# Weight tiles of a block in two halves, 128 bytes apart modulo 256, with the K tiles sorted by the slot parity of their activations

## The chip, the cores and the metric

The kernel runs on one core of one Trainium2 chip. TensorE (PE) multiplies, VectorE (DVE), ScalarE (ACT) and GpSimd (POOL) work element by element, SyncE (SP) issues most of the DMAs. SBUF is the on-chip memory of 128 partitions; a tile has the same byte address in all of them, and the addresses below are those bytes within a partition. Metric: device time in microseconds (us) of one execution, the median over several.

## The reference

One decoder layer for 256 tokens of width 2048, with 16 meta tokens put in front (272 tokens, batch 1, everything in float32):

```python
q, c_kv, q_idx, k_idx, w_idx, u = split_columns(h @ w_in[l])
c_kv = rms_norm(c_kv, kv_norm_g[l])
o_lat = dsa_attention(q_abs, c_kv, q_idx, k_idx, w_idx, rel_bias, top_k)   # top-64 keys per query
pool_out = multiscale_pool(u, w_pool[l], pool_scale[l])
mix = jnp.concatenate([attn_out, pool_out], axis=-1) @ w_o[l]
h = layer_norm(ALPHA * h + mix, ln1_g[l], ln1_b[l])
f = conv_gated_ffn(h, w_up[l], conv_w[l], conv_b[l], w_down[l])   # 2048 -> 2 x 5632 -> 2048
h = layer_norm(ALPHA * h + f, ln2_g[l], ln2_b[l])
```

The large products have K = 2048 (the projections with 24 column blocks of 128 beside the first 336 columns, `w_o` with 16, `w_up` with 88) or K = 5632 (`w_down`).

## The kernel before

Each fp32 matrix is split into a high and a low part of type fp32r (`split_part`, L114 on ACT writes the high part, L115 on DVE the rest), activations and weights alike. A product of a 128 x 128 weight tile with the activations then takes three matmuls: high x high (L219), high x low (L220), low x high (L221). `product` runs them for the 16 K tiles of a block, one K tile after the other: 48 matmuls into one PSUM tile. In these products the weights are the stationary operand, loaded by an LDWEIGHTS of 128 columns ahead of each matmul (engine PEld in the profile), and the activations stream through in 256 to 272 columns. While one matmul streams, the weights of the next are loaded.

The weights come as a stream of blocks of 128 x 2048 floats (1 MB each), in this order: 8 blocks of indexer queries ("qi"), `w_uk` and `w_uv`, 8 blocks of attention queries ("q"), 8 blocks of pool channels ("u"), 16 of `w_o` ("o"), then 88 of `w_up` with the blocks of `w_down` between them (`ffn_plan`). `weights` fetches two blocks ahead: `fetch` (L118) issues one DMA on SP's queue into a tile `wraw` and splits it in two pieces of 1024 columns. The first 4 x 2 blocks of `w_up` multiply `folded` (the attention result before its norm is finished, 260 columns), the other 80 multiply `h_parts` (`hp`, 258 columns). Most of `w_down` runs through a seven-product scheme (`seven`, L812 to L814), where the weights stream in 512 columns and the activations are stationary.

Where things lie:

- `split_tile` (L138) gives a weight block a tile `whl` of 2 parts x 2064 floats, 16,512 bytes. That is 64.5 x 256, so the three buffers of the tag lie at 192, 64 and 192 modulo 256. The low part lies 8,256 bytes (64 modulo 256) behind the high part. K tile k lies at column 128 k, so 512 k bytes further: all 16 K tiles of a block lie alike modulo 256.
- After the three buffers comes a tile `gap` of 64 bytes, then a ring of 24 slots for activations of 2 parts x 272 floats, 2,176 bytes each. That is 8.5 x 256, so slots with an even number lie at 128 and those with an odd number at 0 modulo 256. The low part again lies 64 further.
- The framework picks the slots by which is free. In the built program of the kernel before, x's K tile 0 has slot 0 and K tile k slot 24 - k; `mix` 0 to 15 have the slots 8, 7, 6, 3, 2, 23, 22, 19, 18, 17, 21, 20, 1, 0, 5, 4; `hp` 0 to 15 have 16, 15, 14, 13, 12, 11, 10, 9, 5, 4, 1, 0, 21, 20, 8, 7.
- The qi products read x from column 16 on (64 bytes in), the q products from column 14 (56 bytes), the u products from column 12, 10, 6 or 0. `mix` and `hp` are read from their start. `folded` lies in another pool, in tiles of 2,080 bytes (32 modulo 256 from one to the next).

The order on each engine is set by the framework's scheduler from the order of the program text and from dependences. `output` (L644) reads `mix` in the fixed order 14, 15, 12, 13, 10, 11, 0 to 9; everywhere else the K tiles run from 0 to 15. The last two of `hp` are written (`normalise`, L726, high part L732 on ACT, low part L733 on DVE) while the first product on `hp` runs.

Of the kernel before, what the change touches and what calls it, by code (L numbers as in the profile page):

```python
# [11 lines left out]
F32 = mybir.dt.float32  # L12
F32R = mybir.dt.float32r
# [4 lines left out]
P = 128  # L18
D = 2048
NM = 16  # L20
S = 256
T = NM + S
Q0 = NM - 2
# [28 lines left out]
def ffn_plan():  # L52

    plan, f0 = [], 0
    for part, n in enumerate(PARTS):
        ups = [("up", f, half_) for f in range(f0, f0 + n) for half_ in range(2)]
        downs = []
        if part:
            chunks = 1 if part - 1 == FAST else 2
            downs = [(kind, part - 1, c, j) for c in range(chunks) for kind in "AB" for j in range(PARTS[part - 1] // 2)]  # L60
        while ups or downs:
            plan += ups[:1] + downs[:1]
            ups, downs = ups[1:], downs[1:]
        f0 += n
    return plan + [("down", FAST, c, g) for c in (1, 3) for g in range(PARTS[FAST] // 4)]


@with_exitstack
def tile_layer(ctx, tc, xt, w_first, w_proj, w_uk, w_uv, w_pool, w_o, w_up, w_down, cols, rows, rel_bias, onehot, out):
# [80 lines left out]
    def emit(i):  # L150
        if i in ready:
            return
        if i == last:

            raw = wp.tile([P, 2048], F32, tag="wraw", name="wraw")
            nc.sync.dma_start(raw, stream[i])
            raws[i] = raw
            ready[i] = []
            for c in range(0, 2048, 256):
                hl = ring.tile([P, 2, 258], F32R, tag="act", name="whl_r", padded_shape=[P, 2, T])  # L160
                nc.scalar.activation(hl[:, 0, :256], raw[:, c:c + 256], AF.Copy)
                nc.vector.tensor_tensor(hl[:, 1, :256], raw[:, c:c + 256], hl[:, 0, :256].bitcast(F32), op=ALU.subtract)
                ready[i].append(hl)
            return
        if i == spare:
            raw = wp.tile([P, 2048], F32, tag="wraw", name="wraw")
            hl = sb.tile([P, 2, 2048 + 2], F32R, tag="y", name="whl_y")
# [30 lines left out]
    def pieces(hl, a, b):  # L198
# [3 lines left out]
            return [(slice(c - a, e - a), hl[c // 256][:, 0, :e - c], hl[c // 256][:, 1, :e - c]) for c, e in cuts]  # L202
        return [(slice(0, b - a), hl[:, 0, a:b], hl[:, 1, a:b])]

    def row_sums(i, hl):

        total = sb.tile([P, 1], F32, name=f"total{i}")
        nc.scalar.activation(raws[i], raws[i], AF.Copy, accum_out=total)
        hi, lo = (hl[-1][:, p, 256:] if isinstance(hl, list) else hl[:, p, 2048:] for p in range(2))
        nc.scalar.activation(hi, total.to_broadcast([P, 2]), AF.Copy)  # L210
        nc.vector.tensor_tensor(lo, total.to_broadcast([P, 2]), hi.bitcast(F32), op=ALU.subtract)

    def product(ps, hl, m, act, lo, hi, ks=range(KT), width=P, k0=0, k1=KT):

        for n in range(k0, k1):
            k = ks[n]
            wh, wl = hl[:, 0, k * width:k * width + m], hl[:, 1, k * width:k * width + m]
            ah, al = act[k][:, 0, lo:hi], act[k][:, 1, lo:hi]
            nc.tensor.matmul(ps, wh, ah, start=n == 0, stop=False)  # L219
            nc.tensor.matmul(ps, wh, al, start=False, stop=False)  # L220
            nc.tensor.matmul(ps, wl, ah, start=False, stop=n == KT - 1)  # L221
# [169 lines left out]
    for j in range(8):  # L391
        hl = weights()
        ps = big()
        product(ps[:, :S], hl, P, x_parts, NM, T, k1=9)
        if j:
            pa_ = small()
            dots(j - 1, qis[j - 1], pa_, (0,))
        product(ps[:, :S], hl, P, x_parts, NM, T, k0=9, k1=12)
        if j:
            dots(j - 1, qis[j - 1], pa_, (1,))  # L400
        product(ps[:, :S], hl, P, x_parts, NM, T, k0=12)
# [81 lines left out]
    for h in range(H):  # L483
        hl = weights()
        ps = big()
        product(ps[:, :NQ], hl, P, x_parts, Q0, T)
        nc.scalar.activation(qt[:, h, :], ps[:, :NQ], AF.Copy)


# [122 lines left out]
    for h in range(H):  # L612
        g, j = 3 - h // 2, h % 2
        if j == 0:
            df = ap_.tile([P, 2, 2, NQ], F32R, name="df", tag="df")
        hl = weights()
        ps = big()
        product(ps[:, :T - starts[g]], hl, P, x_parts, starts[g], T, k1=4)
        if h == 0:
            meta_weights()  # L620
        lg_next = softmax(h + 1) if h + 1 < H else None
        product(ps[:, :T - starts[g]], hl, P, x_parts, starts[g], T, k0=4, k1=7)
        if turned:
            values(h - 1, *turned)
        product(ps[:, :T - starts[g]], hl, P, x_parts, starts[g], T, k0=7, k1=9)
        turned = turn(h, lg)
        product(ps[:, :T - starts[g]], hl, P, x_parts, starts[g], T, k0=9, k1=12)
# [6 lines left out]
        product(ps[:, :T - starts[g]], hl, P, x_parts, starts[g], T, k0=12)  # L634
        mean = trailing_mean(g, j, df, ps)
        if j == 1:
            late = (g, df, wpl)
        lg = lg_next
# [5 lines left out]
    def output(m):  # L644
        hl = weights()
        ps = big()
        product(ps[:, :NQ], hl, P, mix, 0, NQ, ks=order, k1=6 if m == 0 else KT)
        if m == 0:
            values(H - 1, *turned)
            less_token(*mean)  # L650
            product(ps[:, :NQ], hl, P, mix, 0, NQ, ks=order, k0=6, k1=14)
            pooled(*late)
            product(ps[:, :NQ], hl, P, mix, 0, NQ, ks=order, k0=14)
# [192 lines left out]
    for item in plan:  # L846
# [48 lines left out]
        if f < FOLDED:  # L895
            k = 0
            if f + half_ == 0:
                product(ps[:, :NE], hl, P, folded, 0, NE, k1=5)
                deviation()
                k = 5  # L900
            product(ps[:, :NE], hl, P, folded, 0, NE, k0=k)
# [209 lines left out]
```

## Time and profile before

| | |
|---|---|
| median of 3 runs | 1042.71 us (1042.28 to 1043.3) |
| profiled execution | 1042.3 us, of which its span is 1040.4 us |
| mean granted TensorE clock | 0.998 |
| PE busy | 1032.5 us (99%) |
| DVE busy | 890.4 us (86%) |
| ACT busy | 619.9 us (60%) |
| HBM read | 232.50 MB |

The span runs from the first instruction to the last one; the profiled execution's own time lies 1.9 us above it. Durations of matmuls overlap, since they are pipelined and their ends are modelled: a matmul's row shows 282 ns, but the next starts some 120 ns later. What a matmul costs is therefore read from start to start, in the timeline.

### The profile page before, as it was taken

The numbers are of one execution on the slowest core, as the hardware profiler recorded it, in microseconds if no ns is written. First come the engines' busy times: TensorE is split into PE (matmuls) and PEld (weight loads), VectorE is DVE, ScalarE is ACT, GpSimd is POOL, SyncE is SP. The second block draws the span as 40 slices with busy tenths as digits, with TensorE's granted clock in tenths as the row PEclk, the third lists the DMA queues.
The fourth block names the chain that finished last, engine by engine and source line by source line (L and its number), as shares of the span: only waits on it lengthen the run. The fifth ranks groups of instructions, "written<-read, shape, count | busy, mean of one in ns | idle before, by whom it ended". The sixth has DMA issues, their size and how long they took to land.

```text
span 1040.4 us, 19199 instructions
## 1 busy us (share of the span) xinstructions
PE 1032.5 (99%) x7644; PEld 984.0 (95%) x7644; DVE 890.4 (86%) x1401; ACT 619.9 (60%) x1000; POOL 186.1 (18%) x245
## 2 busy tenths in 40 slices
PE   9999999999999999999999999999999999999997
PEld 8999999999999999999999999999999999999986
DVE  6879568758779998888999999989898999999876
ACT  7656446645439855555665556655556565556675
POOL 1200014125330021121121111211112101120031
PEclk9999999999999999999999999999999999999999
DMA  9755643354553578989887798877988778888765
GB/s 326 256 183 202 237 145 126 139 194 163 179 194 129 197 224 239 276 282 301 275 276 264 268 294 276 279 264 270 291 279 276 266 280 277 277 274 280 288 218 156
DMA packets 59754, 250.28 MB, mean 241 GB/s; under 512 B 21734, under 2 KB 22416, under 8 KB 32656
## 3 DMA queue, kind: packets, MB, share of 16 engines
q1 hardware_dynamic: 34592, 230.42, 61.4%
q0 software_dynamic: 7888, 16.14, 8.3%
q10 hardware_dynamic: 17184, 2.49, 1.5%
q8 instruction: 60, 0.98, 0.4%
q14 instruction: 30, 0.25, 0.1%
HBM read 232.50 MB, written 2.11 MB: 225 GB/s over the span
## 4 chain that ended last, share of the span: by engine, by line
PE 94%; issue 2%; DMA 1%; DVE 1%; POOL 1%; ACT 0%; SPq 0%; POOLq 0%; DVEq 0%; ACTq 0%
PE mm L220 24%; PE mm L219 24%; PE mm L221 23%; PE at L814 6%; PE at L812 6%; PE at L813 6%; PE mm L291 2%; DMA wraw<-in_w_down 1%; DVE whl L115 1%; POOL gb L931 0%; DMA wraw<-in_w_first 0%; PE mm L519 0%; PE at L554 0%; PE at L381 0%; PE at L380 0%
## 5 line engine op out<-in xcount | busy, mean ns | idle before, releaser
L115 DVE TENSOR_TENSOR whl<-wraw,whl 128x1024 fp32r<-128x1024 f32 (+1 forms) x416 | 486.4, 1203 | 40.7 <-ACT whl L114 40.1
L114 ACT ACTIVATE whl<-wraw 128x1024 fp32r<-128x1024 f32 (+1 forms) x416 | 402.5, 1014 | 102.3 <-DMA wraw<-in_w_up 25.1
L220 PE MATMUL mm<-hp,whl 128*128 128x258 f32 x1280 | 364.3, 285 | 0.0
L219 PE MATMUL mm<-hp,whl 128*128 128x258 f32 x1280 | 361.0, 282 | 0.0
L221 PE MATMUL mm<-hp,whl 128*128 128x258 f32 x1280 | 360.3, 282 | 0.0
L219 PEld LDWEIGHTS mm<-hp,whl 128*128 128x128 f32 x1280 | 242.5, 189 | 3.1
L220 PEld LDWEIGHTS mm<-hp,whl 128*128 128x128 f32 x1280 | 241.6, 189 | 3.4 <-DVE hp L733 0.2
L221 PEld LDWEIGHTS mm<-hp,whl 128*128 128x128 f32 x1280 | 243.4, 190 | 0.2
L219 PE MATMUL mm<-xp,whl 128*128 128x256 f32 (+5 forms) x384 | 112.2, 292 | 0.0
L220 PE MATMUL mm<-xp,whl 128*128 128x256 f32 (+5 forms) x384 | 109.0, 284 | 0.0
L221 PE MATMUL mm<-xp,whl 128*128 128x256 f32 (+5 forms) x384 | 108.8, 283 | 0.0
L747 ACT ACTIVATE z<-mm,cv 128x256 f32<-128x256 f32 x40 | 22.6, 564 | 99.4 <-PE mm L221 97.8
L784 POOL TENSOR_TENSOR forms<-za 128x128 f32<-128x128 f32 x20 | 21.8, 1091 | 312.5 <-DVE za L765 246.0
L219 PEld LDWEIGHTS mm<-xp,whl 128*128 128x128 f32 x384 | 72.5, 189 | 1.0 <-issue 0.5
L220 PEld LDWEIGHTS mm<-xp,whl 128*128 128x128 f32 x384 | 72.4, 189 | 0.4
L221 PEld LDWEIGHTS mm<-xp,whl 128*128 128x128 f32 x384 | 72.4, 188 | 0.0
L747 ACT ACTIVATE za<-mm,cv 128x256 f32<-128x256 f32 x40 | 22.6, 564 | 81.7 <-PE mm L221 74.0
L814 PE MATMUL at<-whl,gp 128*128 128x512 f32 x180 | 71.0, 395 | 0.0
L813 PE MATMUL at<-whl,gp 128*128 128x512 f32 x180 | 70.7, 394 | 0.0
L812 PE MATMUL at<-whl,gp 128*128 128x512 f32 x180 | 69.3, 395 | 0.0
L787 POOL TENSOR_TENSOR forms<-za 128x128 f32<-128x128 f32 x20 | 19.4, 972 | 198.9 <-DVE za L765 184.9
L814 PEld LDWEIGHTS at<-whl,gp 128*128 128x128 f32 x180 | 33.8, 188 | 7.9
(349 smaller groups left out, 1886.7 us busy)
## 6 DMA issues: line engine op xcount, KB each, us to landing
wraw<-in_w_up SPq DMA_DIRECT2D x88, 1024.0 KB, 5.1
wraw<-in_w_down SPq DMA_DIRECT2D x80, 1024.0 KB, 6.6
wraw<-in_w_proj SPq DMA_DIRECT2D x24, 1024.0 KB, 5.1
wraw<-in_w_o SPq DMA_DIRECT2D x16, 1024.0 KB, 4.9
y<-v POOLq DMA_DIRECT2D x27, 256.0 KB, 7.7
y<-u POOLq DMA_DIRECT2D x18, 256.0 KB, 4.9
wraw<-in_w_first SPq DMA_DIRECT2D x8, 304.0 KB, 5.3
x<-in_xt SPq DMA_DIRECT2D x1, 2176.0 KB, 8.1
```

What stands on the lines that cost most here:

```text
L114: upper = nc.scalar.activation(hl[:, 0, c], raw[:, c], AF.Copy)
L115: lower = nc.vector.tensor_tensor(hl[:, 1, c], raw[:, c], hl[:, 0, c].bitcast(F32), op=ALU.subtract)
L219: nc.tensor.matmul(ps, wh, ah, start=n == 0, stop=False)
L220: nc.tensor.matmul(ps, wh, al, start=False, stop=False)
L221: nc.tensor.matmul(ps, wl, ah, start=False, stop=n == KT - 1)
L291: nc.tensor.matmul(ps[:m, :T], hl[:, t // 2, a0 + a:a0 + a + m], x_parts[k][:, t % 2, :], start=k == 0 and t == 0, stop=k == KT - 1 and t ...
L747: nc.scalar.activation(z, src[:, 2:NQ], AF.Identity, bias=col(C_B, j), scale=col(C_W, 3 * j + 2))
L784: nc.gpsimd.tensor_tensor(s[:, 0], a21, a22, op=ALU.add)
L787: nc.gpsimd.tensor_tensor(s[:, 3], a11, a21, op=ALU.subtract)
L812: nc.tensor.matmul(ps, a[:, 0, i], hl[:, 0, w], start=j == 0, stop=False)
L813: nc.tensor.matmul(ps, a[:, 0, i], hl[:, 1, w], start=False, stop=False)
L814: nc.tensor.matmul(ps, a[:, 1, i], hl[:, 0, w], start=False, stop=j == n - 1)
```

## The change

The change concerns `whl` and the order of K tiles in it.

- `whl` becomes 2 halves x 2 parts x 1040 floats, 16,640 bytes (65 x 256), so all three buffers lie alike modulo 256. The second half begins 8,320 bytes (128 modulo 256) behind the first, the low part 4,160 bytes (64 modulo 256) behind the high part. A small class `Split` lets the code index it as before.
- The host orders the K tiles of `w_proj`, `w_o` and `w_up` by three lists. The first eight of a list lie in the first half, the others in the second. In `K_O` and `K_UP` the first eight are the K tiles whose activations have even slots; in `K_PROJ` they are those with odd slots.
- `product` takes the list (`places`) to find a tile and by default also runs in its order. `output` keeps its order; the last of the u products keeps 0 to 15; the first product on `hp` runs in the order of `K_UP` with 14 and 15 last (`late_last`).
- The first stage (L243 ff.) places its six weight pieces of a buffer three to a half.
- To make room, `lm` shares the tag of `work`, and the four sums of `row_sums` share a tile `totals`. That moves the weight buffers and the ring: 96 bytes fewer stand ahead of them, and each weight buffer is 128 bytes larger.

The number of instructions, DMAs and bytes stays what it was.

```diff
+class Split:
+    def __init__(self, tile):
+        self.tile = tile
+    def __getitem__(self, key):
+        rows, part, c = key
+        a, b = c.start, 2 * 1024 + 2 if c.stop is None else c.stop
+        at = int(a >= 1024)
+        assert b <= 1024 or at == 1
+        return self.tile[rows, at, part, a - 1024 * at:b - 1024 * at]
+
+K_PROJ = (1, 3, 5, 7, 9, 11, 13, 15, 0, 2, 4, 6, 8, 10, 12, 14)
+K_O = (0, 2, 4, 6, 8, 11, 13, 15, 1, 3, 5, 7, 9, 10, 12, 14)
+K_UP = (0, 2, 4, 6, 9, 11, 13, 14, 1, 3, 5, 7, 8, 10, 12, 15)
...
-        hl = wp.tile([P, 2, 2048 + 2], F32R, tag="whl", name="whl", padded_shape=[P, 2, 2064])
+        hl = Split(wp.tile([P, 2, 2, 1024 + 16], F32R, tag="whl", name="whl"))
...
+    totals, totalled = sb.tile([P, 4], F32, name="totals"), []
+
     def row_sums(i, hl):
-        total = sb.tile([P, 1], F32, name=f"total{i}")
+        total = totals[:, len(totalled):len(totalled) + 1]
+        totalled.append(i)
...
-    def product(ps, hl, m, act, lo, hi, ks=range(KT), width=P, k0=0, k1=KT):
+    def product(ps, hl, act, lo, hi, places, ks=None, k0=0, k1=KT):
         for n in range(k0, k1):
-            k = ks[n]
-            wh, wl = hl[:, 0, k * width:k * width + m], hl[:, 1, k * width:k * width + m]
+            k = (places if ks is None else ks)[n]
+            w = slice(P * places.index(k), P * places.index(k) + P)
+            wh, wl = hl[:, 0, w], hl[:, 1, w]
...
-            xk, wk, c = raw[:, k % 3, :T], raw[:, k % 3, T:], slice(k % 6 * MF, k % 6 * MF + MF)
+            xk, wk, a0 = raw[:, k % 3, :T], raw[:, k % 3, T:], k % 6 // 3 * 1024 + k % 3 * MF
+            c = slice(a0, a0 + MF)
...
-    work = ap_.tile([P, KW], F32, name="work")
+    work = ap_.tile([P, KW], F32, name="work", tag="work")
...
-    lm = ap_.tile([2, H, NM], F32, name="lm")
+    lm = ap_.tile([P, KW], F32, name="lm", tag="work")[:2, :H * NM].rearrange("p (a b) -> p a b", b=NM)
...
+        ks = range(KT) if h == H - 1 else None
+        product(ps[:, :T - starts[g]], hl, x_parts, starts[g], T, K_PROJ, ks, k1=4)
...
-        product(ps[:, :NQ], hl, P, mix, 0, NQ, ks=order, k1=6 if m == 0 else KT)
+        product(ps[:, :NQ], hl, mix, 0, NQ, K_O, ks=order, k1=6 if m == 0 else KT)
...
+    late_last = [k for k in K_UP if k < 14] + [14, 15]
...
-            product(ps[:, :NQ], hl, P, h_parts, 0, NQ)
+            product(ps[:, :NQ], hl, h_parts, 0, NQ, K_UP, ks=late_last if f == FOLDED else None)
...
-    def blocks(w):
+    def blocks(w, places):
         k, m = w.shape
-        return np.ascontiguousarray(w.reshape(k // P, P, m // P, P).transpose(2, 1, 0, 3)).reshape(m // P, P, k)
+        w = w.reshape(k // P, P, m // P, P)[list(places)]
+        return np.ascontiguousarray(w.transpose(2, 1, 0, 3)).reshape(m // P, P, k)
```

More of the change, by code (lines that the diff above doesn't have):

```diff
@@ L166, in emit @@
             raw = wp.tile([P, 2048], F32, tag="wraw", name="wraw")
-            hl = sb.tile([P, 2, 2048 + 2], F32R, tag="y", name="whl_y")
+            hl = Split(sb.tile([P, 2, 2, 1024 + 16], F32R, tag="y", name="whl_y"))
         else:
@@ L393, in tile_layer @@
         ps = big()
-        product(ps[:, :S], hl, P, x_parts, NM, T, k1=9)
+        product(ps[:, :S], hl, x_parts, NM, T, K_PROJ, k1=9)
         if j:
@@ L397, in tile_layer @@
             dots(j - 1, qis[j - 1], pa_, (0,))
-        product(ps[:, :S], hl, P, x_parts, NM, T, k0=9, k1=12)
+        product(ps[:, :S], hl, x_parts, NM, T, K_PROJ, k0=9, k1=12)
         if j:
             dots(j - 1, qis[j - 1], pa_, (1,))
-        product(ps[:, :S], hl, P, x_parts, NM, T, k0=12)
+        product(ps[:, :S], hl, x_parts, NM, T, K_PROJ, k0=12)
         qi = queries[:, j % 2]
@@ L485, in tile_layer @@
         ps = big()
-        product(ps[:, :NQ], hl, P, x_parts, Q0, T)
+        product(ps[:, :NQ], hl, x_parts, Q0, T, K_PROJ)
         nc.scalar.activation(qt[:, h, :], ps[:, :NQ], AF.Copy)
@@ L617, in tile_layer @@
         ps = big()
-        product(ps[:, :T - starts[g]], hl, P, x_parts, starts[g], T, k1=4)
+        ks = range(KT) if h == H - 1 else None
+        product(ps[:, :T - starts[g]], hl, x_parts, starts[g], T, K_PROJ, ks, k1=4)
         if h == 0:
@@ L621, in tile_layer @@
         lg_next = softmax(h + 1) if h + 1 < H else None
-        product(ps[:, :T - starts[g]], hl, P, x_parts, starts[g], T, k0=4, k1=7)
+        product(ps[:, :T - starts[g]], hl, x_parts, starts[g], T, K_PROJ, ks, k0=4, k1=7)
         if turned:
             values(h - 1, *turned)
-        product(ps[:, :T - starts[g]], hl, P, x_parts, starts[g], T, k0=7, k1=9)
+        product(ps[:, :T - starts[g]], hl, x_parts, starts[g], T, K_PROJ, ks, k0=7, k1=9)
         turned = turn(h, lg)
-        product(ps[:, :T - starts[g]], hl, P, x_parts, starts[g], T, k0=9, k1=12)
+        product(ps[:, :T - starts[g]], hl, x_parts, starts[g], T, K_PROJ, ks, k0=9, k1=12)
         if j == 1:
@@ L633, in tile_layer @@
             less_token(*mean)
-        product(ps[:, :T - starts[g]], hl, P, x_parts, starts[g], T, k0=12)
+        product(ps[:, :T - starts[g]], hl, x_parts, starts[g], T, K_PROJ, ks, k0=12)
         mean = trailing_mean(g, j, df, ps)
@@ L650, in output @@
             less_token(*mean)
-            product(ps[:, :NQ], hl, P, mix, 0, NQ, ks=order, k0=6, k1=14)
+            product(ps[:, :NQ], hl, mix, 0, NQ, K_O, ks=order, k0=6, k1=14)
             pooled(*late)
-            product(ps[:, :NQ], hl, P, mix, 0, NQ, ks=order, k0=14)
+            product(ps[:, :NQ], hl, mix, 0, NQ, K_O, ks=order, k0=14)
         yd = y[:, m, Q0:]
@@ L897, in tile_layer @@
             if f + half_ == 0:
-                product(ps[:, :NE], hl, P, folded, 0, NE, k1=5)
+                product(ps[:, :NE], hl, folded, 0, NE, K_UP, k1=5)
                 deviation()
                 k = 5
-            product(ps[:, :NE], hl, P, folded, 0, NE, k0=k)
+            product(ps[:, :NE], hl, folded, 0, NE, K_UP, k0=k)
             with behind(state["use"]):
@@ L1085 @@
         "w_first": np.concatenate([tokens.T.reshape(KT, P, T), first.reshape(KT, P, MF)], axis=2),
-        "w_proj": blocks(np.concatenate([qi, q] + [u[:, 256 * g:256 * g + 256] for g in (3, 2, 1, 0)], axis=1)),
+        "w_proj": blocks(np.concatenate([qi, q] + [u[:, 256 * g:256 * g + 256] for g in (3, 2, 1, 0)], axis=1), K_PROJ),
         "w_uk": a["w_uk"][0].reshape(2, P, 1024).transpose(1, 0, 2).reshape(P, 2048),
@@ L1089 @@
         "w_pool": a["w_pool"][0].reshape(4, 2, P, 256).transpose(0, 2, 1, 3).reshape(4, P, 512),
-        "w_o": blocks(a["w_o"][0]),
-        "w_up": blocks(a["w_up"][0]),
+        "w_o": blocks(a["w_o"][0], K_O),
+        "w_up": blocks(a["w_up"][0], K_UP),
         "w_down": np.concatenate(down, axis=0),
```

## The prediction

> **What bounds the kernel.** I read the page's busy times and its chain of waits first, then a window over the long feed-forward stretch, then PE's groups of instructions, and last PE's timeline row by row.
>
> ```profile
> PE 1032.5 (99%) x7644; PEld 984.0 (95%) x7644; DVE 890.4 (86%) x1401; ACT 619.9 (60%) x1000; POOL 186.1 (18%) x245
> PE 94%; issue 2%; DMA 1%; DVE 1%; POOL 1%; ACT 0%; SPq 0%; POOLq 0%; DVEq 0%; ACTq 0%
> ```
>
> ```profile
> 350.00:1004.00 654.00, 653.96 (x4674) 617.17 (x4673) 596.96 (x843) 388.99 (x557) 104.67 (x125) 1.00 0.82 272
> ```
>
> In the window the columns are the stretch, its length, then busy us of PE, PEld, DVE, ACT and POOL, the granted clock, DMA share and GB/s. PE is on 94% of the chain and without a gap in 654 us, at full clock: a nanosecond less per matmul is a nanosecond less in the span, as long as DVE (596.96 of 654, 91%) and the DMAs (0.82) follow. So the question is only what a matmul costs from start to start.
>
> ```profile
> L220 PE MATMUL mm<-hp,whl 128*128 128x258 f32 x1280 | 364.3, 285 | 0.0
> L219 PE MATMUL mm<-hp,whl 128*128 128x258 f32 x1280 | 361.0, 282 | 0.0
> L221 PE MATMUL mm<-hp,whl 128*128 128x258 f32 x1280 | 360.3, 282 | 0.0
> L219 PE MATMUL mm<-xp,whl 128*128 128x256 f32 (+5 forms) x384 | 112.2, 292 | 0.0
> L220 PE MATMUL mm<-mixa,whl 128*128 128x258 f32 x128 | 36.5, 285 | 0.0
> L813 PE MATMUL at<-whl,gp 128*128 128x512 f32 x180 | 70.7, 394 | 0.0
> ```
>
> The products on `hp` are 80 blocks of 16 K steps of three matmuls; those on x and on `mix` (half `mixa`, half `mixp`) are 24 and 16 blocks. Now two successive `hp` products in the timeline, the first matmul of each K step (start us, us, the rest names it). The first product's weights lie in a buffer at 192 modulo 256:
>
> ```profile
> 897.58 0.28 PE L219 MATMUL mm<-hp,whl 128*128 128x258 f32 x1
> ...
> 897.94 0.28 PE L219 MATMUL mm<-hp,whl 128*128 128x258 f32 x1
> ...
> 898.29 0.29 PE L219 MATMUL mm<-hp,whl 128*128 128x258 f32 x1
> ...
> 898.66 0.28 PE L219 MATMUL mm<-hp,whl 128*128 128x258 f32 x1
> ...
> 899.02 0.28 PE L219 MATMUL mm<-hp,whl 128*128 128x258 f32 x1
> ...
> 899.38 0.28 PE L219 MATMUL mm<-hp,whl 128*128 128x258 f32 x1
> ...
> 899.74 0.28 PE L219 MATMUL mm<-hp,whl 128*128 128x258 f32 x1
> ...
> 900.10 0.28 PE L219 MATMUL mm<-hp,whl 128*128 128x258 f32 x1
> ...
> 900.45 0.28 PE L219 MATMUL mm<-hp,whl 128*128 128x258 f32 x1
> ```
>
> The second product's weights lie in the middle buffer, at 64:
>
> ```profile
> 905.43 0.28 PE L219 MATMUL mm<-hp,whl 128*128 128x258 f32 x1
> ...
> 905.78 0.29 PE L219 MATMUL mm<-hp,whl 128*128 128x258 f32 x1
> ...
> 906.15 0.28 PE L219 MATMUL mm<-hp,whl 128*128 128x258 f32 x1
> ...
> 906.51 0.28 PE L219 MATMUL mm<-hp,whl 128*128 128x258 f32 x1
> ...
> 906.87 0.28 PE L219 MATMUL mm<-hp,whl 128*128 128x258 f32 x1
> ...
> 907.23 0.28 PE L219 MATMUL mm<-hp,whl 128*128 128x258 f32 x1
> ...
> 907.59 0.28 PE L219 MATMUL mm<-hp,whl 128*128 128x258 f32 x1
> ...
> 907.94 0.29 PE L219 MATMUL mm<-hp,whl 128*128 128x258 f32 x1
> ...
> 908.31 0.28 PE L219 MATMUL mm<-hp,whl 128*128 128x258 f32 x1
> ```
>
> K steps 0, 2, 4, 6 have even slots, 1, 3, 5, 7 odd ones. In the first product the even steps take 0.36, 0.37, 0.36, 0.36 (1.45 us) and the odd ones 0.35, 0.36, 0.36, 0.35 (1.42). In the second the even ones take 1.42 and the odd ones 1.46. The roles are swapped with the buffer, so neither the slot nor the buffer sets the time, but the distance between the two. I call "offset" the address of the streamed activations less that of the weight tile that is loaded meanwhile (the next matmul's), modulo 256. Even slots lie at 128, odd ones at 0: the offset is 192 for even and 64 for odd slots in the first product, the other way round in the second. Offset 192 is the slow one in both. High and low parts both lie 64 further, so within a K step the offset stays.
>
> I then grouped all K steps in this way, start to start. The first and last rows of the groups: 384 steps on x, 256 on `mix`, 1280 on `hp`:
>
> ```profile
> 23.39 0.28 PE L219 MATMUL mm<-xp,whl 128*128 128x256 f32 x1
> ...
> 207.21 0.28 PE L221 MATMUL mm<-xp,whl 128*128 128x260 f32 x1
> 207.33 0.28 PE L219 MATMUL mm<-mixp,whl 128*128 128x258 f32 x1
> ...
> 302.17 0.28 PE L221 MATMUL mm<-mixp,whl 128*128 128x258 f32 x1
> ...
> 350.16 0.28 PE L219 MATMUL mm<-hp,whl 128*128 128x258 f32 x1
> ...
> 984.48 0.28 PE L221 MATMUL mm<-hp,whl 128*128 128x258 f32 x1
> ```
>
> For `hp` and `mix` the means of the three matmuls are 118.2, 120.5 and 117.8 ns at offset 64 (356.5 a step) and 119.3, 123.6 and 120.2 at 192 (363.1): 6.6 ns between them, the same in all three buffers. Half of the steps have each, whatever the buffer.
>
> **The change part by part.** First the layout. The three buffers become 3 x 16,640 bytes (0 modulo 256) and the gap stays 64, so even slots lie 64 behind the first half of any buffer and odd ones 192; to the second half it is 192 and 64. `K_O` and `K_UP` put even slots in the first half and odd ones in the second: every step gets 64. `K_PROJ` does the reverse: 192, plus where x is read from.
>
> Products on `hp`: 8 of 16 steps go from 363.1 to 356.5, 52.8 ns a block. Where the order passes from one half to the other, one third matmul meets a weight tile of the other half: 2.4 back. 50.4 ns x 80 blocks = 4.0 us.
>
> Products on `mix`: the first two matmuls of 8 steps gain 1.1 + 3.1 each, 33.6 ns a block. But `output` keeps its order, in which 14 of 15 passes change halves, so nearly all third matmuls get 192 where half of them had it: 7 x 2.4 = 16.8 ns back. 16.8 ns x 16 = 0.3 us.
>
> Products on x: offsets 0 and 128 (qi, 355.9 and 356.7 ns a step), 248 and 120 (q, 361.6 and 364.1) and four pairs in u whose differences of -1.0 to +4.2 ns nearly cancel. With `K_PROJ` they stay at 0, at 248 and at u's 192 to 240: about 0.1 us gained in all, of bounds +-0.3.
>
> The first eight products on `folded` already run through all offsets in steps of 32, and still do: 0. The 756 matmuls of 512 columns (L812 to L814) stream the weights instead; grouped by offset their steps lie between 229 and 235 ns, and the mean over the new offsets is the old one: 0, with +-1 ns each, +-0.8 us, as bounds. First stage and the end: the same instructions, 0. Host order, `totals` and `lm`: no instruction more; the tiles share storage on engines that run in order there, 0, and DVE's free time covers a wait.
>
> A loss: the order at the first product on `hp`.
>
> ```profile
> 352.05 0.77 DVE L733 TENSOR_TENSOR hp<-x,hp 128x258 fp32r<-128x258 f32 x2
> ...
> 355.40 0.42 DVE L733 TENSOR_TENSOR hp<-x,hp 128x258 fp32r<-128x258 f32 x1
> ```
>
> ```profile
> 355.56 0.28 PE L219 MATMUL mm<-hp,whl 128*128 128x258 f32 x1
> 355.88 0.39 PE L220 MATMUL mm<-hp,whl 128*128 128x258 f32 x1
> ```
>
> These are the low parts of `hp` 13 and 14, then of 15. PE waits 0.2 us for the last already (0.32 instead of 0.12). Now 13 comes seventh, due at 350.16 + 6 x 0.36 + 0.12 = 352.44 while the pair of DVE's ends at 352.82; and PE comes earlier by what it has gained. Queued behind PE's wait are the next products, whose weights lie ready. At worst the product ends when it did, and the 0.4 us of the x and `mix` products and 0.05 of this one are lost; at best DVE comes earlier too, and nothing is. I take 0.3, nearer the worst, since this DVE row is no reply to PE.
>
> Sum: 4.0 + 0.3 + 0.1 - 0.3 = 4.1 us. Against the profiled execution's 1042.3 that is 1038.2; the median of the runs is 0.4 higher, so I say 1038.6. Of this kernel no measurement tells less than about 0.2% (2.1 us) from no change.
>
> The Trainium skill (TensorE: Matmul & The Clock Gate, "Step-by-step: what each phase is for") speaks against all this: TensorE has two independent SBUF read ports, and loading the next tile's weights takes no read bandwidth from the running matmul. By that the offset could not matter and the sum would be 0. The trace disagrees here: 6.6 ns a step, with the sign swapped by the buffer.
>
> **The rivals.** (1) No change: the offset is noise, or a slow step's delay is given back to the next one, so that alternation hides that the sum is fixed. For it: the steps all take 0.35 to 0.37 us, a small spread. Against it: the swap above, and that slots 9 and 5 (K steps 7 and 8) and 20 and 8 (13 and 14) follow each other with the same parity: the second of two fast steps still takes 357.0 ns, that of two slow ones 361.6. At most 2 ns of the 6.6 are given back. Time 1042.7. This is also what the two-port rule gives.
>
> (2) Slower: the scheduler hands out the slots otherwise in the new program, and the lists sort by the wrong parity. One `hp` K tile in the wrong half costs 80 x 6.6 ns = 0.53 us; at 8 of 16 the gain on `hp` is gone, from 12 on the kernel is slower by over 2.1 us, and with all 16 the sum turns round: 1042.7 + 4.4 = 1047. For it: the lists are fixed numbers while the slots are found anew. Against it: slots come free in the order in which K tiles are last read, and that order is kept where it counts (the last u product, `output`).
>
> (3) DVE takes half back: it is 91% busy, and with PE's blocks 0.6% shorter it is at 92%; a split that comes late would show as PE gaps. In 654 us there are 0.04 us of such gaps now. Half the gain: 1040.6.
>
> **How the numbers follow.** The forecast 0.78, (1) 0.07, (2) 0.07, (3) 0.08. The likeliest case's own range is 1036 to 1040.5: up, less the `mix` and x terms and 0.8 for the 512 columns and 0.5 for what is given back; down, 355 a step as in the faster of the rows above (16 x 4.8 ns x 80 = 6.1 us). Faster has the forecast and half of (3), 0.82; same 0.11; slower 0.07. The range to hold 8 in 10 reaches up to no change: 1035.8 to 1042.8.
>
> **What would show it.** In the profile after, the mean of the `hp` groups should go from 285 and 282 to 283 (L220) and 281 or 280 (L219, L221); the steps of one `hp` product should be 0.35 and 0.36 throughout, in every buffer; the span should be 1036.3, with PE's groups of 512 columns still at 394 to 396. At `hp`'s first product a PE wait of 0.2 to 0.6 us on L733 should stand. The forecast is wrong if odd or even steps are still at 0.365 (slots), if all steps are at 0.36 or more (given back), or if PE gaps before the weights appear.

## The result and the profile after

The changed kernel takes 1041.32 us in the median (1040.3 to 1042.33), the kernel before 1042.98 us (1042.22 to 1044.61) beside it on the same chip. The ratio is 0.9983 with a 95% interval of 0.9976 to 0.9989: the change gains 1.7 us. Forecast were 1038.6 us and a gain of 4.1. The sign is right, the size less than half.

From the page of the kernel after (the span, the busy times of the engines, the shares of the chain that ended last, PE's groups):

```profile
span 1039.4 us, 19199 instructions
PE 1032.3 (99%) x7644; PEld 982.6 (95%) x7644; DVE 891.0 (86%) x1401; ACT 621.2 (60%) x1000; POOL 186.9 (18%) x245
PE 97%; issue 2%; POOL 1%; DMA 0%; ACT 0%; POOLq 0%; SPq 0%; ACTq 0%
L245 PE MATMUL mm<-hp,whl 128*128 128x258 f32 x1280 | 362.5, 283 | 0.0
L247 PE MATMUL mm<-hp,whl 128*128 128x258 f32 x1280 | 360.3, 282 | 0.0
L246 PE MATMUL mm<-hp,whl 128*128 128x258 f32 x1280 | 360.1, 281 | 0.0
```

L245, L246 and L247 are now the three matmuls of a K step (L219 to L221 before). PE still bounds the kernel and has no gap in the `hp` groups. Its second matmul fell from 285 to 281 ns, but the first rose from 282 to 283 and the third stands at 282, as before. Counted from start to start, which is what the span feels, the three took 118.7, 122.0 and 119.05 ns before (359.8 a step) and take 120.7, 119.2 and 119.0 now (358.9). The forecast had 356.5.

How a step comes out is seen in one `hp` product of the timeline after, in which every step has the offset 64 (first matmuls of K steps 6 to 13; start us, us):

```profile
898.22 0.29 PE L245 MATMUL mm<-hp,whl 128*128 128x258 f32 x1
...
898.58 0.28 PE L245 MATMUL mm<-hp,whl 128*128 128x258 f32 x1
...
898.93 0.28 PE L245 MATMUL mm<-hp,whl 128*128 128x258 f32 x1
...
899.30 0.28 PE L245 MATMUL mm<-hp,whl 128*128 128x258 f32 x1
...
899.65 0.29 PE L245 MATMUL mm<-hp,whl 128*128 128x258 f32 x1
...
900.02 0.28 PE L245 MATMUL mm<-hp,whl 128*128 128x258 f32 x1
...
900.37 0.29 PE L245 MATMUL mm<-hp,whl 128*128 128x258 f32 x1
...
900.74 0.28 PE L245 MATMUL mm<-hp,whl 128*128 128x258 f32 x1
```

The steps take 0.36, 0.35, 0.37, 0.35, 0.37, 0.35, 0.37: although all lie alike, they alternate by themselves, and a pair takes 0.72 us, as a slow and a fast one did before. Over all 80 products the step means by their place in the product are 355.1, 357.2, 358.5, 359.1, 359.5, 359.5, 359.6 and 359.7 ns in the first half, and 357.4 to 360.7 in the second. So the first steps after the 512-column matmuls are cheap, and from the fifth on a step costs about what the mean of slow and fast was before, 359.8.

The stretch of `up` and `down` goes from the first matmul on `hp` to the last. The rows of the timeline after:

```profile
349.19 0.28 PE L245 MATMUL mm<-hp,whl 128*128 128x258 f32 x1
...
982.95 0.29 PE L247 MATMUL mm<-hp,whl 128*128 128x258 f32 x1
```

That is 633.76 us; before it was 634.32 (984.48 less 350.16). By the starts of the first matmuls of the stages in the two profiled executions, 1040.4 and 1039.4 us long:

| stage | after less before, us |
|---|---|
| start and first product | -0.02 |
| qi and its neighbours (x, offset 0) | -0.34 |
| q (x, offset 248) | -0.54 |
| u (x) | +0.13 |
| `mix` products | -0.30 |
| `folded` products | +0.12 |
| up and down stretch | -0.56 (products on `hp` -1.08, the 512-column matmuls on `right` +0.57) |
| last `down` matmuls, and those of the last norm (L1032) | +0.91 |
| after the last matmul | -0.40 |

The sum is -1.0; the medians of many runs differ by 1.7, and single runs of one kernel spread by 2 us. The stages repeat better than the whole: q gains 0.54 us in all of the runs below that have this layout, sorted x and the gap of 64, but for the one with fewer weights loaded. So the gain that can be placed lies as much on x and `mix` as on `hp`, on which nearly all of the forecast lay.

### The profile page after: what moved, and what is told of

Read it like the earlier page. It is cut to its first block, busy times and chain, and to the rows that moved or that the text cites. A ratio compares the mean times of both kernels' runs of the same rounds, so it can differ in the third digit from the quotient of the medians.

```text
span 1039.4 us, 19199 instructions
## 1 busy us (share of the span) xinstructions
PE 1032.3 (99%) x7644; PEld 982.6 (95%) x7644; DVE 891.0 (86%) x1401; ACT 621.2 (60%) x1000; POOL 186.9 (18%) x245
## 4 chain that ended last, share of the span: by engine, by line
PE 97%; issue 2%; POOL 1%; DMA 0%; ACT 0%; POOLq 0%; SPq 0%; ACTq 0%
PE mm L245 24%; PE mm L247 24%; PE mm L246 24%; PE at L842 6%; PE at L844 6%; PE at L843 6%; PE mm L318 2%; PE mm L894 1%; PE mm L896 1%; PE mm L895 1%; POOL gb L961 0%; PE mm L546 0%; PE at L581 0%; PE at L407 0%; PE at L408 0%
## 5 line engine op out<-in xcount | busy, mean ns | idle before, releaser
L245 PE MATMUL mm<-hp,whl 128*128 128x258 f32 x1280 | 362.5, 283 | 0.0
L247 PE MATMUL mm<-hp,whl 128*128 128x258 f32 x1280 | 360.3, 282 | 0.0
L246 PE MATMUL mm<-hp,whl 128*128 128x258 f32 x1280 | 360.1, 281 | 0.0
L246 PEld LDWEIGHTS mm<-hp,whl 128*128 128x128 f32 x1280 | 243.1, 190 | 3.2
L245 PEld LDWEIGHTS mm<-hp,whl 128*128 128x128 f32 x1280 | 241.8, 189 | 3.2
L247 PEld LDWEIGHTS mm<-hp,whl 128*128 128x128 f32 x1280 | 241.8, 189 | 0.2
L245 PE MATMUL mm<-xp,whl 128*128 128x256 f32 (+5 forms) x384 | 111.7, 291 | 0.0
L246 PE MATMUL mm<-xp,whl 128*128 128x256 f32 (+5 forms) x384 | 108.7, 283 | 0.0
L247 PE MATMUL mm<-xp,whl 128*128 128x256 f32 (+5 forms) x384 | 108.6, 283 | 0.0
L245 PEld LDWEIGHTS mm<-xp,whl 128*128 128x128 f32 x384 | 72.4, 189 | 1.0 <-issue 0.5
L246 PEld LDWEIGHTS mm<-xp,whl 128*128 128x128 f32 x384 | 72.4, 189 | 0.4
L247 PEld LDWEIGHTS mm<-xp,whl 128*128 128x128 f32 x384 | 72.3, 188 | 0.0
```

## The experiments

My theory after the result: the 356.5 ns that the kernel before shows for offset 64 are not the price of that offset, but the price of such a step behind one of the other kind. In a run of like steps the price settles, within about three steps, at another value. The rivals: the lists sort the wrong way round; the price is a fixed rate that no order and no place can move; the layout, and not the order, brought what was gained.

All runs in one table. Each ratio is against the kernel before on the same chip, whose median there was 1043.07 us (order_only, swapped, unsorted, gap0), 1042.96 us (gap32, gap96, off248, less_load) or 1042.56 us (layout_alone, runs4, off120, off248_mix), so medians of different rows compare only roughly. "Step" is the mean from start to start of a K step on `hp`, "stretch" the up and down stretch less that of the kernel before (634.32 us).

| run | offset on `hp` | median us | ratio (95%) | step ns | stretch us |
|---|---|---|---|---|---|
| before | 64 and 192 in turn | 1042.98 | | 359.8 | |
| after | 64 | 1041.32 | 0.9983 (0.9976 to 0.9989) | 358.9 | -0.56 |
| order_only | runs of 64, of 192 | 1044.5 | 1.0012 (1.0003 to 1.0021) | 361.0 | +1.45 |
| swapped | 192 | 1045.78 | 1.0032 (1.0019 to 1.0044) | 363.1 | +3.38 |
| unsorted | 64 and 192 in turn | 1041.19 | 0.9981 (0.9972 to 0.9991) | 359.7 | -0.84 |
| layout_alone | 64 and 192 in turn | 1042.12 | 0.9996 (0.9987 to 1.0005) | as unsorted | -0.84 |
| runs4 | runs of four | 1043.64 | 1.001 (1.0001 to 1.0019) | 360.3 | +0.87 |
| gap0 | 0 | 1046.42 | 1.0033 (1.002 to 1.0045) | 362.8 | +3.02 |
| gap32 | 32 | 1049.96 | 1.0069 (1.0056 to 1.0082) | 365.7 | +7.36 |
| gap96 | 96 | 1042.13 | 0.999 (0.9981 to 0.9999) | 360.1 | -0.33 |
| off120 | 120 | 1042.23 | 0.9998 (0.9989 to 1.0007) | 360.0 | +0.30 |
| off248 | 248 | 1039.3 | 0.9969 (0.9957 to 0.9981) | 358.1 | -2.51 |
| off248_mix | 248 | 1039.65 | 0.9975 (0.9964 to 0.9986) | as off248 | -2.50 |
| less_load | 64 | 1036.03 (a single run) | | 356.9 | -4.07 |

**The order without the layout.** The kernel before, its buffers as they were; the products on x, `folded` and `hp` run through the slots of one parity first:

```
+K_PROJ = (1, 3, 5, 7, 9, 11, 13, 15, 0, 2, 4, 6, 8, 10, 12, 14)
+K_UP = (0, 2, 4, 6, 9, 11, 13, 14, 1, 3, 5, 7, 8, 10, 12, 15)
...
-            product(ps[:, :NQ], hl, P, h_parts, 0, NQ)
+            product(ps[:, :NQ], hl, P, h_parts, 0, NQ, ks=late_last if f == FOLDED else K_UP)
```

> The order alone: weight blocks lie as in the kernel before, but the products on x, folded and hp run the K steps of one slot parity first and then those of the other, so that offsets 192 and 64 come in runs of eight instead of alternating. Own-price theory (that of the prediction: each matmul has a price by its own offset): in the hp products the steps at offset 64 stay at 356.5 ns and those at 192 at 363.1, the time stays at 1043.0 within 0.5. Rhythm theory (the stream of matmuls settles in a rhythm of about 120 ns a matmul, and a change of offset only moves delay from one step to the next): from the third or fourth step of a run on, both runs stand at 359 to 361 ns, within 2 ns of each other; the time is 1042 to 1043, slightly better than before since runs start fast.

Each step keeps its offset, and only its neighbours change. The first and last `hp` rows of its timeline:

```profile
350.67 0.28 PE L223 MATMUL mm<-hp,whl 128*128 128x258 f32 x1
...
986.43 0.28 PE L225 MATMUL mm<-hp,whl 128*128 128x258 f32 x1
```

The stretch is 635.76 us, 1.45 longer than before, and the kernel 0.12% slower (0.03 to 0.21). The steps at 64 now cost 358.5 ns (356.5 before), those at 192 363.5 (363.1). Sorting alone takes something away, because the fast steps lose 2.0 ns and the slow ones gain nothing. So the price of a step depends on the steps before it. Neither reading had foretold this: the two kinds stand 5 ns apart, where the rhythm reading allowed 2, and the time is above both ranges. In the q stage, with its offsets 248 and 120, the same sorting gains 0.47 us, so whether runs are cheap is a matter of their offset.

**The other offset throughout.** The halves of two lists of the changed kernel exchanged:

```
-K_O = (0, 2, 4, 6, 8, 11, 13, 15, 1, 3, 5, 7, 9, 10, 12, 14)
-K_UP = (0, 2, 4, 6, 9, 11, 13, 14, 1, 3, 5, 7, 8, 10, 12, 15)
+K_O = (1, 3, 5, 7, 9, 10, 12, 14, 0, 2, 4, 6, 8, 11, 13, 15)
+K_UP = (1, 3, 5, 7, 8, 10, 12, 15, 0, 2, 4, 6, 9, 11, 13, 14)
```

> The changed kernel with the halves of the lists for w_o and w_up exchanged: all steps on hp have offset 192 instead of 64, the first two matmuls of those on mix too. Own-price theory: hp steps at 363.1 ns instead of the 358.9 measured after, 80 x 16 x 4.2 = 5.4 us more, time 1046 to 1048. Rhythm theory: hp steps settle at 359.7 as with offset 64, time 1040.5 to 1042.5.

Its PE groups on `hp`, from its page:

```profile
L246 PE MATMUL mm<-hp,whl 128*128 128x258 f32 x1280 | 364.5, 285 | 0.0
L247 PE MATMUL mm<-hp,whl 128*128 128x258 f32 x1280 | 363.6, 284 | 0.0
L245 PE MATMUL mm<-hp,whl 128*128 128x258 f32 x1280 | 359.5, 281 | 0.0
```

The second and third matmuls stand at 285 and 284 where the change has 281 and 282. A step takes 363.1 ns from start to start, and the kernel is slower than before by 2.7 us. So the lists of the change sort the right way round, and the settled price is no fixed rate: 192 throughout costs 4.2 ns a step more than 64 throughout. Here every tile lies where it lies in the changed kernel, and only which slot meets which half of the weights differs, so the distance between the two counts and not the address of either.

**The layout without the order.** First `w_o` and `w_up` in plain order, with x still sorted; then all three lists plain:

```
-K_O = (0, 2, 4, 6, 8, 11, 13, 15, 1, 3, 5, 7, 9, 10, 12, 14)
-K_UP = (0, 2, 4, 6, 9, 11, 13, 14, 1, 3, 5, 7, 8, 10, 12, 15)
+K_O = tuple(range(16))
+K_UP = tuple(range(16))
```

> The changed kernel with w_o and w_up stored and run in the order 0 to 15: the layout alone for these, so offsets 64 and 192 alternate on hp as before. Own-price theory: back to 356.5 and 363.1 in turn; against the changed kernel as predicted 4.0 us more, against it as measured 1.0 us. Rhythm theory: the same alternation, 1.0 to 1.4 us above the changed kernel, 1042.4 to 1042.8, with the 0.5 to 0.8 us from the products on x kept.

```
-K_PROJ = (1, 3, 5, 7, 9, 11, 13, 15, 0, 2, 4, 6, 8, 10, 12, 14)
+K_PROJ = tuple(range(16))
...
+K_O = tuple(range(16))
+K_UP = tuple(range(16))
```

> The changed kernel with all three lists set to 0 to 15: only the two halves of the block are left, no sorting anywhere. If the gain of the whole change comes from the sorted runs on x (0.5 us in q, found in every kernel with sorted x), this gives that back against the kernel with w_o and w_up unsorted: 1041.7 to 1042.0. If the layout by itself is what gained, 1041.2 as there.

The first and last `hp` rows of unsorted:

```profile
349.39 0.28 PE L245 MATMUL mm<-hp,whl 128*128 128x258 f32 x1
...
982.87 0.28 PE L247 MATMUL mm<-hp,whl 128*128 128x258 f32 x1
```

The stretch is 633.48 us, 0.28 less than in the changed kernel. With `w_up` unsorted the steps on `hp` alternate again, 356.8 ns at offset 64 and 362.6 at 192, and the time is 1041.19 us: that of the whole change. Both readings had put it 1.0 us or more above. Counted with the last matmul of each product, the steps on `hp` do take 0.5 us more than in the changed kernel. But the 512-column matmuls on `right`, which the changed kernel has 0.57 us slower than before, take 0.25 us less than before here; why is open. Ordering `w_o` and `w_up` by parity, the main part of the change, is worth nothing that can be measured. With x unsorted too the time is 1042.12, and q's gain is gone (-0.08 us instead of -0.54). The layout alone does not differ from the kernel before (0.9987 to 1.0005). What remains as the source of the gain is the order on x in the new layout. The traces show it in q; in the whole time the intervals of these two runs still overlap by a little.

**Run lengths.** The kernel before, its `hp` order in four runs of four:

```
+RUNS = (0, 2, 4, 6, 1, 3, 5, 7, 9, 11, 13, 14, 8, 10, 12, 15)
...
-            product(ps[:, :NQ], hl, P, h_parts, 0, NQ)
+            product(ps[:, :NQ], hl, P, h_parts, 0, NQ, ks=range(KT) if f == FOLDED else RUNS)
```

> The kernel before with only the order of the hp products changed (not the first): four K steps of one slot parity, four of the other, twice. Own-price theory: nothing changes, 359.8 ns a step in the mean, 1043.0. Settled-price theory (a step's price moves over some three steps from that in alternation to that of its run, 359.7 at offset 64 and 363.3 at 192): the mean lies between 359.8 for runs of one and 361.2 for runs of eight, about 360.5, so 0.5 to 1.5 us above the kernel before.

Mostly single steps (before) 359.8 ns, runs of four 360.3, runs of eight (order_only) 361.0: the longer the runs, the more of the steps have the settled price. Within a run of four the steps at 64 take 351.5, 357.5, 357.8 and 360.6 ns, the first of them behind a run at 192; in the runs of eight of order_only they begin with 352.5, 357.2, 357.9 and 360.2 and stay there, while those at 192 stand at 363 to 364 from the start. That is what a memory of a few steps makes, and a price that hung on the step's own offset alone would not move at all.

**Other offsets, by one tile's size.** The gap tile between the weight buffers and the ring is 64 bytes a partition. Left out, or 32 or 96 bytes, it moves the ring and the pools behind it against the weight buffers, and changes nothing else:

```
-            wp.tile([P, 16], F32, tag="gap", name="gap", bufs=1)
+            wp.tile([P, 8], F32, tag="gap", name="gap", bufs=1)
```

That is the one of 32; the one of 96 has `[P, 24]`, and the one of 0 no such line.

> The changed kernel without the 64-byte tile between weight buffers and ring: every offset is 64 less, 0 on hp, 192 to 128 on x. Own-price theory: from the rows on x of 256 columns (0 and 128 within 0.8 ns a step) offset 0 lies about midway between 64 and 192, so hp steps of 359 to 360 ns, 1041 to 1043. Rhythm theory: steps that settle at 359.7 within 1, time 1040.5 to 1042.5. A time outside these would say that like offsets do have a rate of their own.

> The changed kernel with 32 bytes between weight buffers and ring instead of 64: offset 32 on hp. If a run of like offsets has a settled price of its own that varies smoothly (0: 363.2, 64: 359.7, 192: 363.3 ns a step), 32 lies between 359 and 364: 80 x 16 x 1.7 = 2 us above the changed kernel, 1043 to 1045. If only runs as such matter and 0 was special, 359.7 and 1041.3.

> The changed kernel with 96 bytes between weight buffers and ring: offset 96 on hp. Settled prices that vary smoothly, with the minimum near 64: 359 to 362 ns a step, 1041 to 1044. A minimum beyond 64 would give 355 to 358 and 1037 to 1040, which would be a better place than that of the change.

The first and last `hp` rows of the timeline with the gap of 32:

```profile
350.44 0.28 PE L245 MATMUL mm<-hp,whl 128*128 128x258 f32 x1
...
992.12 0.29 PE L247 MATMUL mm<-hp,whl 128*128 128x258 f32 x1
```

The stretch is 641.68 us: the same instructions in the same order, with the activations 32 bytes nearer to the weights, take 7.9 us longer than in the changed kernel. Late in a run (from the fifth step of each half of a product on), a step on `hp` takes 366 to 367 ns on average here, at offset 0 363, at 96 359.9. These are averages: by their place in the product, the later steps lie between 364 and 369 ns at 32 and between 357 and 363 at 96. My guess of one settled value for all offsets falls, and so does that of a smooth course: 32 is dearer than both 0 and 64, and the time of 1049.96 us lies far above the 1043 to 1045 that it gave.

**Offset 248.** In q, runs at 248 had come out well (358.4 ns a step with sorted x, 362.8 in turn before). So the halves of `K_UP` are exchanged, and `hp` is written and read from column 14 on (`Q0`, 56 bytes further):

```
-K_UP = (0, 2, 4, 6, 9, 11, 13, 14, 1, 3, 5, 7, 8, 10, 12, 15)
+K_UP = (1, 3, 5, 7, 8, 10, 12, 15, 0, 2, 4, 6, 9, 11, 13, 14)
...
-        nc.scalar.activation(a[:, 0, :NQ], yd, AF.Copy)
-        nc.vector.tensor_tensor(a[:, 1, :NQ], yd, a[:, 0, :NQ].bitcast(F32), op=ALU.subtract)
+        nc.scalar.activation(a[:, 0, Q0:], yd, AF.Copy)
+        nc.vector.tensor_tensor(a[:, 1, Q0:], yd, a[:, 0, Q0:].bitcast(F32), op=ALU.subtract)
...
-            product(ps[:, :NQ], hl, h_parts, 0, NQ, K_UP, ks=late_last if f == FOLDED else None)
+            product(ps[:, :NQ], hl, h_parts, Q0, T, K_UP, ks=late_last if f == FOLDED else None)
```

> The changed kernel with the halves of the list for w_up exchanged and hp written and read from column 14 on, as x is in the q products: all steps on hp have offset 248. In the q products a run at 248 takes 358.4 ns a step (119.4, 119.8, 119.2) in the changed kernel, against 362.8 in the mean before. If the settled price belongs to the offset, hp falls from 358.9 to 358.4 a step, 0.6 us below the changed kernel: 1040 to 1041.5. If it belongs to the place in the program, hp at 248 lies where 192 and 0 lie, 363: 1045 to 1047.

The first and last `hp` rows of its timeline:

```profile
349.98 0.28 PE L245 MATMUL mm<-hp,whl 128*128 128x258 f32 x1
...
981.79 0.29 PE L247 MATMUL mm<-hp,whl 128*128 128x258 f32 x1
```

631.81 us, 2.5 less than before and 1.9 less than in the changed kernel; 1.0 of the 1.9 is the steps on `hp` (358.1 for 358.9 ns, 1280 times), the rest the 512-column matmuls between them. Late in a run a step takes 356.7 ns on average (356 to 358 by place). At 1039.3 us this version is the fastest of those that do the whole computation, 0.31% (0.19 to 0.43) faster than before. Two more kernels test whether it is column 14 itself, and whether `mix` gains in the same way. In the first `hp` lies as here, but `K_UP` is that of the change, so the offset is 120; the second has the edit of off248 and also moves `mix` to column 14 and exchanges the halves of `K_O`.

> The changed kernel with hp written and read from column 14 on, lists unchanged: offset 120 on hp, the only difference to off248 being 128 bytes. Settled-price theory, between 96 (359.9) and what x showed at 120 in the kernel before (364 a step, in alternation with 248): 358 to 364 a step, 1041 to 1046. If reading from column 14 was the gain of off248 and not the offset: 356.7 a step and 1039.3 again.

> off248 with the same done for mix: written and read from column 14, halves of w_o's list exchanged, so the first two matmuls of a step on mix have offset 248 and, since the fixed order passes from half to half, the third mostly 120. If offset 248 helps in matmuls of any product: 0.3 to 0.8 us below off248, 1038.5 to 1039.2. If the third at 120 takes it back: 1039.3 to 1040.

At offset 120 a step costs 360.0 ns and the gain is gone, so the column alone isn't it. All tiles lie alike in these two kernels, and only the pairing of slots and halves differs. `mix` got worse: 0.36 us longer than before, where the change has it 0.30 shorter. The third matmul of a step did not take it back, at 119.4 ns; the first did, at 122.1 where the change has 119.9. The order on `mix` changes halves at nearly every step, so it has no runs of one offset, and nothing says that it should follow the settled prices.

**Fewer weights loaded.** The changed kernel; the second matmul of each step loads 32 of 128 weight columns:

```
-            nc.tensor.matmul(ps, wh, al, start=False, stop=False)
+            nc.tensor.matmul(ps[:32], wh[:, :32], al, start=False, stop=False)
```

> The changed kernel in which the second matmul of every K step loads only 32 of the 128 weight columns (so the output leaves out three quarters of the high x low terms). Its load runs beside the first matmul of the step. Collision theory (the load takes read time from the streaming matmul, and the offset says when they meet): the first matmul's 120.7 ns on hp falls by several ns, to 108 to 116; the second and third, beside which 128 columns are loaded, change less. Two-port theory (load and stream do not touch): the first matmul stays at 120 to 121 ns and only the instruction's own time shrinks.

From its page, matmuls and weight loads on `hp`:

```profile
L245 PE MATMUL mm<-hp,whl 128*128 128x258 f32 x1280 | 357.4, 279 | 0.0
...
L247 PEld LDWEIGHTS mm<-hp,whl 128*128 128x128 f32 x1280 | 242.4, 189 | 12.2
L245 PEld LDWEIGHTS mm<-hp,whl 128*128 128x128 f32 x1280 | 242.0, 189 | 3.2
L246 PEld LDWEIGHTS mm<-hp,whl 128*32 128x32 f32 x1280 | 138.5, 108 | 3.7 <-DVE hp L763 0.5
```

The small load takes 108 ns instead of 189 (L246). The matmul beside which it runs is the first of the step (L245): it falls from 283 to 279 ns, and from start to start from 120.7 to 117.2; the other two rise by 0.9 and 0.6 (120.1 and 119.6). The stretch shrinks by a further 3.5 us against the change, 2.6 of it by the steps (2.0 ns, 1280 times). So what is loaded meanwhile is one part of a matmul's price, 3.5 ns of 120.7 for three quarters of a load. That is the way of the collision reading, but short of its 108 to 116 ns. It is a single run, and it doesn't tell whether the first matmul streams faster or the second may start sooner because its smaller load is done sooner; the second also writes 32 rows of output instead of 128.

## Why the prediction was right and wrong

**Layout and lists: right.** By the addresses of the built program the slots were handed out as before, even ones at 160 and odd ones at 32 modulo 256, all three buffers at 96; every step on `hp` has the offset 64. Rival (2) fell, and the exchanged halves (1045.78 us) show that its sign was right; the cost was 2.7 us, and not the 4.3 up to its 1047.

**The failed step** is "8 of 16 steps go from 363.1 to 356.5, 52.8 ns a block", 4.0 us in all. Measured are 0.9 ns a step over all 16, 1.08 us in all. The 363.1 and 356.5 were right as a description of the kernel before, and came back with the layout unsorted (362.6 and 356.8). But a step at 64 is at 356.5 behind one at 192; behind its own kind it goes to 359.7 within three or four steps. So the price of a pattern was taken for the price of a place.

Rival (1) named just this ("a slow step's delay is given back to the next one") and got 0.07. It was struck down by one look: the second of two like fast steps still took 357.0 ns, so "at most 2 ns of the 6.6 are given back". That row was true, and after it the price rises further: 355.1, 357.2, 358.5, 359.1, 359.5. Two steps were too few to see where it ends, and no product on `hp`, `mix` or x in the kernel before had more. The prediction could have said that the run is an unknown, with 359.8 as its other end. Rival (1) does not hold in full either, since the sum of two steps isn't fixed: 192 throughout costs 363.1 and 248 throughout 358.1.

By the Trainium skill's rule (TensorE: Matmul & The Clock Gate, "Step-by-step: what each phase is for") the place could not matter. The traces disagree again, by 7.9 us in the `up` and `down` stretch between two kernels that differ in one gap by 32 bytes. The rule gave 1042.7, which is 1.4 us from what was measured, against 2.7 for my sum: nearer, but not for its reason.

**Products on `mix`:** forecast -0.3, measured -0.30, and that is luck. The first matmul takes 119.9 ns, not 118.2, and the third, at 192, takes 118.2, not 120.2. On `hp` too the third matmul at the switch of halves costs 0.7 ns more than the others, not 2.4.

This bears on what "offset" means. The prediction counts the distance to the weights loaded meanwhile, those of the next matmul. Only at a switch of halves do these lie otherwise than the weights of the step itself, and there the price does not follow them: in the unsorted kernel, behind two matmuls at 192, a third matmul takes 120.6 ns when the next weights put it at 64 and 120.9 when they put it at 192, while at 64 behind two matmuls at 64 it takes 118.9. So that the next weights are what counts is not shown. It may be those of the step itself, or the matmuls before; no run separates the two.

**Products on x:** forecast "about 0.1 us", bounds +-0.3; measured -0.75 over qi, q and u (-0.34, -0.54, +0.13), outside the bounds. I had priced q as I had `hp`, by the means in turn, and here the runs settle lower than that. That this is the order's doing is shown by q's -0.47 in order_only and -0.08 in layout_alone. In qi neither alone gains (+0.32 and +0.08); only layout and order together do.

**`folded`:** forecast 0, measured +0.12. **512 columns:** forecast 0 with bounds of 0.8; measured +0.57 on `right`, within them. Behind the stretch 0.91 us more are lost. Some 0.5 of it is one wait that the kernel before doesn't have, in the last `down` products (PE's rows after):

```profile
1016.97 0.28 PE L1048 MATMUL mm<-whl,gp 128*128 128x258 f32 x1
1017.52 0.39 PE L1049 MATMUL mm<-whl,gp 128*128 128x258 f32 x1 [0.26 <-DVE whl L236]
```

The second matmul starts 0.55 us after the first, instead of 0.12: DVE is late with the low part of the row sums (L236, in `row_sums`). The prediction had put row sums and DVE there at 0. Not every kernel with this layout has the wait (off248 has not, -0.04), so it hangs on when DVE and PE get there, and the layout alone doesn't make it.

**The loss of 0.3 at the first product on `hp`** did not come. The DVE rows and the two PE waits after:

```profile
350.98 0.77 DVE L763 TENSOR_TENSOR hp<-x,hp 128x258 fp32r<-128x258 f32 x2
...
354.33 0.43 DVE L763 TENSOR_TENSOR hp<-x,hp 128x258 fp32r<-128x258 f32 x1
```

```profile
351.47 0.39 PE L246 MATMUL mm<-hp,whl 128*128 128x258 f32 x1
351.69 0.29 PE L247 MATMUL mm<-hp,whl 128*128 128x258 f32 x1
...
354.81 0.39 PE L246 MATMUL mm<-hp,whl 128*128 128x258 f32 x1
355.04 0.28 PE L247 MATMUL mm<-hp,whl 128*128 128x258 f32 x1
```

In place of one PE wait of 0.2 to 0.6 there are two waits of 0.1 us (0.22 and 0.23 instead of 0.12), at 13 and at 15, where before 0.2 and 0.1 were lost at 15. The product starts 0.97 us earlier (349.19 for 350.16) and DVE's last row comes 1.07 earlier (354.33 for 355.40). "This DVE row is no reply to PE" did not hold; the other end, "DVE comes earlier too, and nothing is" lost, held.

**Rival (3)**, gaps before the weights that take half the gain, fell on `hp`: 0.0 us of idle time in the three groups. The one wait above is of its kind, DVE late with a split part, though not where it was looked for.

## What to carry to other kernels

A price that is read from steps in turn holds for steps in turn: before an order is changed, look for runs of at least four like steps in the trace, and if there are none, keep the mean of the pattern as one end of the range. Try the order alone and the layout alone; here the one lost some 1.4 us, the other gained nothing that can be measured, and what paid, as far as it can be placed, was the order on x, the smallest term of the sum. Where matmuls with fresh weights follow each other without a gap, the place of the weights against the activations modulo 256 is worth a search by a gap tile: between gaps of 32 and 64 bytes this kernel moved by 8.6 us, from 1049.96 to 1041.32.

## What the runs showed of the hardware

A K step of three matmuls of 258 columns, each with a weight load of its own, has a price that hangs on the distance between activations and weights. Late in a run of like steps its average is 356.7 ns at offset 248, 359.7 at 64, 359.9 at 96, about 360 at 120, about 363 at 0, 363 to 364 at 192, 366 to 367 at 32. That is nearly 3% between the ends, at a granted clock of 0.997 to 0.998. Only at 64 do the averages by place come to rest, within 1 ns (359.5 to 360.3); at 120 they swing between 355 and 364.

The price has a memory of about three steps, seen most plainly at 64 behind 192 (352 to 353, 357, 358, then 360 ns). After 512-column matmuls it starts low (355.1 ns at offset 64) and climbs, and in a run of like steps single ones still alternate between 0.35 and 0.37 us.

Loading 32 weight columns instead of 128 brings the start of the next matmul 3.5 ns nearer to that of the one that streams meanwhile (one run). The Trainium skill has it that TensorE never waits for anyone at SBUF (SBUF — State Buffer, "Who interferes with whom"); whichever part of it holds for other engines, TensorE's activations and weights are not free of each other here: exchanging which halves meet which slots, all else alike, moved the step by 4.2 ns. Where they meet, which weights count, and what remembers three steps, no run shows; it stays open.
